# Softmax weights of mixer A's second-layer heads: turned by VectorE's 32x32 blocks and the DRAM instead of by TensorE, with their transfers on SyncE

## The chip, the cores and the metric

The kernel runs on one core of a Trainium2 chip. The metric is the device time of one execution in microseconds (us); lower is better. TensorE (PE) does the matrix products, VectorE (DVE), ScalarE (ACT) and GpSimd (POOL) the work between them, and SyncE (SP) issues the transfers (DMAs). Each engine takes its instructions in a fixed order, and an instruction that waits holds up those behind it on its engine. That order is set when the program is built, by a scheduler that sorts the instructions of each engine.

## The reference, cut to what matters

Two layers, each of a parallel mixer and a gated MLP, on 256 tokens of width 2048 in float32. In the mixer one projection gives queries, keys and values for mixer A (8 heads, windowed, a learned sink logit, 2 key/value heads) and mixer B (8 heads, neighbourhood attention with a bias), and a gate for each.

```
q, k normalised, a part of them rotated            # mixer A, per head of 128
s = q k^T * scale, masked to |i-j| <= 128
m = max(max_k s, sink)
p = exp(s - m);  p = p / (sum_k p + exp(sink - m)) # softmax weights, 256 x 256
o = p v
# mixer B: the same with a bias table in place of the mask and without the sink
x = x + gate * (out_proj(gA * proj_A(oA) + gB * proj_B(oB)))
x = x + gate * down(silu-gated, convolved up-projection)
```

For `o = p v` TensorE needs p with the keys on the partitions. The scores come out with the queries there, so each head's p (two tiles of 128 x 256) has to be turned.

## The kernel before, in words

**The weight stream.** The weights are read once, in units of 1 MB (16 blocks of 128 x 128; `unit_steps`, load `w` in L325 on SP). The pool of raw tiles holds four, shared with the rows `aw` of the adaptive-norm projection (L231), so a load is issued when an earlier unit's last reader is done. A unit is split in two halves: ACT casts a half to its upper part `hl[:, 0]` (L336), DVE subtracts for the lower part `hl[:, 1]` (L337), and the half lies in a ring of four. TensorE makes three products of each block (L355 to L357 for a block that gives features, L418 to L420 for one that gives tokens): the first, and for features the second too, needs only the upper part; the others need DVE's.

**Work beside the stream.** After each unit the stream calls `Paced.tick`: first the functions that `later(n, ...)` put off by n units, then the background jobs at their rates. The attention is such a job: `attention()` starts the eight heads of mixer A (`head_a`) and the eight of mixer B (`head_b`) in turn, and each of its steps moves every head that has begun by one `yield`. `ATT` is its rate for the two layers, `ATT_B` the rate once mixer A's projection is reached. Program order made in this way is what the scheduler starts from.

**A head** (`attend`, L643 on): scores `sc` on TensorE (L648, 6 products), the maxima with mask or bias on DVE (L651) and their negation `nm` (L656), exponentials with their sums on ACT (L659), for mixer A the sink's share (L662, L663), the reciprocal `ri` on DVE (L665), the scaling on ACT (L667), a `yield`, the turn, and then `po` on TensorE (L697), whose result goes to `oA` or `oB` through ACT and DVE (L699, L700).

**The turn.** By TensorE: four transposes to a PSUM tile `tp` (L689), which `split` brings to `pT` with a cast on ACT (L430) and a subtraction on DVE (L431) of 128 x 512. By blocks (`turned_blocks`): DVE transposes each of the two 128 x 256 tiles in blocks of 32 x 32 (L313) into two rows of storage; eight DMAs of 32 KB take them to a DRAM tile `pY` with the blocks exchanged (L316, issued by POOL); two DMAs of 128 KB on SP bring them back (`read_back`, L299); and `split` works on two pieces of 128 x 256. Each read-back is made to wait for `halved[0]`, the DVE split (L337) of the weight half that was emitted last at that point, so that SP's queue takes it no earlier. `BACK` says how many units the read-back is put off. `MOVED` lists, per layer, how many heads of mixers A and B are turned by blocks: in the kernel before none of the first layer, and of the second mixer B's eight.

**Also near:** q and k of later groups are normalised in the same stretch of the second layer: sums of squares on ACT (L588), `qss` on DVE (L481), the power on POOL (`qrs`, L482), `qn` on DVE (L597), transposes `qtp` on TensorE (L621), `packB` on ACT (L622). Each head's split of q, k and v is an ACT/DVE pair of 128 x 256 (L430, L431). The bias of a head of mixer B is loaded to its `p` by SP, 256 KB. `sc`, `po`, `tp` and `qtp` share one PSUM pool (`ax`).

Of the kernel before, what the change touches and what calls it, by code (L numbers as in the profile page):

```python
# [9 lines left out]
F32 = mybir.dt.float32  # L10
# [5 lines left out]
P = 128  # L16
L = 2
D = 2048
S = 256
# [12 lines left out]
BLOCK = 32  # L32
# [47 lines left out]

H_RATE = [2.7, 1.7]

ATT = [1.288, 0.4]
ATT_B = [0.21, 0.4]

SCORES_3 = (1,)

BACK = [3, 4]
MOVED = [(0, 0), (0, 8)]

ADA_ORDER = [[p * KC + k for k in range(KC) for p in ps] for ps in ((0, 1), (2,), (3, 4), (5,))]
ADA_ORDER = [i for part in ADA_ORDER for i in part]
# [47 lines left out]
def encoder(ctx: ExitStack, tc: tile.TileContext, a: dict, out: bass.AP):  # L140
    nc = tc.nc
# [18 lines left out]
    dram = pool("dram", 2, space=bass.MemoryType.DRAM)  # L160
# [126 lines left out]
    def once(fn):  # L287

        due = [fn]

        def run():
            if due:
                due.pop()()

        return run

    def read_back(dst, src):

        tc.add_manual_dep(nc.sync.dma_start(dst, src).ins, halved[0], BEHIND)  # L299

    def later(n, fn):

        if n == 0:
            fn()
        else:
            bg.defer(lambda: later(n - 1, fn))

    def turned_blocks(p, rows, n, tag):

        y = dram.tile([P, n, S], F32, name=tag, tag=tag)  # L310
        to = y[:].rearrange("(b i) n (t a j) -> t a i n b j", i=BLOCK, t=2, a=P // BLOCK)
        for t, row in enumerate(rows):
            nc.vector.transpose(out=row, in_=p[t])  # L313
            src = row.rearrange("p (n b j) -> p n b j", n=n, j=BLOCK)
            for a in range(P // BLOCK):
                nc.gpsimd.dma_start(to[t, a], src[a * BLOCK : (a + 1) * BLOCK])  # L316
        return y

    def unit_steps(l, u, by_halves=False):

# [106 lines left out]
    def split(dst, src, scale=None):  # L427

        if scale is None:
            nc.scalar.copy(dst[:, 0], src)  # L430
            nc.vector.tensor_tensor(out=dst[:, 1], in0=src, in1=dst[:, 0].bitcast(F32), op=ALU.subtract)  # L431
            return
        nc.scalar.activation(out=dst[:, 0], in_=src, func=AF.Copy, scale=scale)
        nc.vector.scalar_tensor_tensor(
            out=dst[:, 1], in0=src, scalar=scale, in1=dst[:, 0].bitcast(F32), op0=ALU.mult, op1=ALU.subtract
        )
# [192 lines left out]
    def in_halves(src, name, tag, yes):  # L629

        if not yes:
            return (src,)
        off = {"vh": ROW - OFF, "qh": 0, "kh": OFF}[tag]
        hl = at.tile([P, 2 * S + off], F32R, name=name, tag=tag, bufs=1)[:, off:]
        halves = hl.rearrange("p (i s) -> p i s", i=2) if len(src.shape) == 2 else hl.rearrange("p (i a s) -> p i a s", i=2, a=2)
        split(halves, src)
        return halves[:, 0], halves[:, 1]

    def by(x):

        return ((0, 0), (0, 1), (1, 0))[: 2 * len(x) - 1]

    def attend(q, k, v, p, mask, scale, sink, o, rows=None):  # L643

        sc = ax.tile([P, 2, S], F32, name="sc", tag="ax")
        for t in range(2):
            for i, j in by(q):
                nc.tensor.matmul(sc[:, t], q[i][:, t * P : (t + 1) * P], k[j], start=i + j == 0, stop=(i, j) == by(q)[-1])  # L648
        m = sm.tile([P, 2], F32, name="m", tag="m")
        for t in range(2):  # L650
            nc.vector.tensor_tensor_reduce(  # L651
                out=p[:, t], in0=sc[:, t], in1=mask[:, t], scale=scale, scalar=-3.0e38 if sink is None else sink,
                op0=ALU.add, op1=ALU.max, accum_out=m[:, t : t + 1],
            )
        nm = sm.tile([P, 2], F32, name="nm", tag="nm")
        nc.vector.tensor_scalar(out=nm[:], in0=m[:], scalar1=-1.0, scalar2=None, op0=ALU.mult)  # L656
        den = sm.tile([P, 2], F32, name="den", tag="den")
        for t in range(2):
            nc.scalar.activation(out=p[:, t], in_=p[:, t], func=AF.Exp, bias=nm[:, t : t + 1], accum_out=den[:, t : t + 1])  # L659
        if sink is not None:  # L660
            es = sm.tile([P, 2], F32, name="es", tag="es")
            nc.scalar.activation(out=es[:], in_=nm[:], func=AF.Exp, bias=sink)  # L662
            nc.vector.tensor_tensor(out=den[:], in0=den[:], in1=es[:], op=ALU.add)  # L663
        ri = sm.tile([P, 2], F32, name="ri", tag="ri")
        nc.vector.reciprocal(out=ri[:], in_=den[:])  # L665
        for t in range(2):
            nc.scalar.activation(out=p[:, t], in_=p[:, t], func=AF.Copy, scale=ri[:, t : t + 1])  # L667
        yield
        if rows is not None:
            rows = rows()  # L670
            y = turned_blocks([p[:, t] for t in range(2)], rows, 2, "pY")

            def back():
                for k in range(2):
                    read_back(rows[k], y[:, k])

            back = once(back)
            later(BACK[sink is None], back)
            yield
            yield  # L680
            back()
            pT = at.tile([P, 2, 2, S], F32R, name="pT", tag="pT", bufs=1)
            for k in range(2):
                split(pT[:, :, k], rows[k])
        else:
            tp = ax.tile([P, 2, S], F32, name="tp", tag="ax")
            for k in range(2):
                for t in range(2):
                    nc.tensor.transpose(tp[:, k, t * P : (t + 1) * P], p[:, t, k * P : (k + 1) * P], ident[:])  # L689
            pT = at.tile([P, 2, 2, S], F32R, name="pT", tag="pT", bufs=1)  # L690
            split(pT, tp[:])
        v = v()
        yield
        po = ax.tile([P, 512], F32, name="po", tag="ax")
        for i, j in by(v):
            for b in range(2):
                nc.tensor.matmul(po[:, :S], v[i][:, b], pT[:, j, b], start=i + j + b == 0, stop=i + b == 2)  # L697
        o = o()
        nc.scalar.copy(o[:, 0], po[:, :S])  # L699
        nc.vector.tensor_tensor(out=o[:, 1], in0=po[:, :S], in1=o[:, 0].bitcast(F32), op=ALU.subtract)  # L700
# [93 lines left out]
    def small(l):  # L794

        if l == 0:
            tables.extend((load(a["maskA"], [P, 2, S], "maskA"), load(a["cs"], [P, 2, 2, HALF], "cs")))
        cs = tables[1]
        gains = load(a["gains"][l], [P, 4], f"gains{l}", lay, tag="gains", bufs=1)
        rg = load(a["rg"][l], [P, 2, ROT], f"rg{l}", lay, tag="rg", bufs=1)  # L800
        sink = load(a["sink"][l], [P, HA], f"sink{l}", lay, tag="sink", bufs=1)
        cw = load(a["cw"][l], [P, 2 * FC, 4], f"cw{l}", lay, tag="cw", bufs=1)
        nc.vector.tensor_scalar(out=gains[:, 2:3], in0=gains[:, 2:3], scalar1=SCALE, scalar2=None, op0=ALU.mult)
        rots = []
        for w in range(2):
            rot = lay.tile([P, 4, 2, HALF], F32, name=f"rot{l}_{w}", tag=f"rot{w}", bufs=1)
            for i, (f, g) in enumerate(((0, 0), (1, 1), (0, 1), (1, 0))):
                nc.vector.tensor_tensor(
                    out=rot[:, i], in0=cs[:, f],
                    in1=rg[:, w, g * HALF : (g + 1) * HALF].unsqueeze(1).broadcast_to([P, 2, HALF]), op=ALU.mult,  # L810
                )
            rots.append(rot)

        return gains, sink, cw, rots

    for l in range(L):
# [41 lines left out]
        def head_a(i):  # L858
# [18 lines left out]
            def rows():  # L877
# [3 lines left out]
            yield from attend(  # L881
                q, k, v, p, tables[0], SCALE, sink[:, i : i + 1], lambda: oA[i], rows if i < MOVED[l][0] else None
            )

        def head_b(hb):
# [8 lines left out]
                q, k, lambda: in_halves(v[:, :, i * HEAD : (i + 1) * HEAD], f"vB{l}_{hb}", "vh", True), p, p, 1.0, None,  # L894
                lambda: oB_of(hb), (lambda: [b[:, 8 + i], b[:, i]]) if hb < MOVED[l][1] else None,
            )

        def oB_of(hb):
            if hb == 0:
                o = place("a", 12, F32R, f"oB{l}_{hb}")  # L900
                oB.extend(o[:, 2 * i : 2 * i + 2] for i in range(6))
            elif hb == 6:
                oB.extend(chunks_of(sp, "b0", 6, f"oB{l}_{hb}", 2))
            return oB[hb]
# [30 lines left out]
        for pi, (groups, gates) in enumerate(parts):  # L935
            last = pi == len(parts) - 1
            for g, part in enumerate(groups):
                have_h(part)
                pss = st.tokens(h, part)
                if pi == max(0, len(parts) - 2) and g == 0:  # L940
                    gains, sink, cw, rots = small(l)
                dst = packs[g // 3][:, 4 * (g % 3) : 4 * (g % 3) + 4]
                rows = dst.rearrange("p (t a) s -> p t (a s)", t=2)
# [25 lines left out]
                if g == 2:  # L969
                    bg.add(job, ATT[l])  # L970

# [29 lines left out]
        for tag in ("y0", "y1", "y2"):  # L1001
            t = place(tag, 4, F32, f"gb{l}_{tag}")
            gb += [t[:, i] for i in range(4)]
        for i in range(2):
            t = paired(F32, f"gb{l}_{i}")
# [56 lines left out]
        for gi, chunks in enumerate(FF_GROUPS):  # L1062
# [34 lines left out]
            for cs in sets:  # L1097
                fns = [lambda p, e=e, c=c: e(p, c) for c in cs for e in (g_evac, v_evac)]
                src = bare.chunks if gi == 0 and cs[0] < BARE[1] // 2 else bare.h
# [113 lines left out]
```

## Time and profile before

| what | before |
|---|---|
| device time, median of 3 runs (lowest to highest) | 2662.33 us (2660.89 to 2663.44) |
| device time of the profiled execution | 2661.44 us |
| its span, first to last instruction | 2659.3 us |
| mean granted TensorE clock | 1.000 |
| busy: PE, DVE, ACT, POOL | 2647.6, 2106.2, 1411.5, 75.0 us |
| HBM read, written | 697.13 MB, 4.19 MB |

The profiled execution takes 2.1 us more than its span and stands 0.9 us below the median of the three runs. The profile's rows name an engine, a line of the kernel, and the tile written and read; "PEld" is TensorE's loading of weights, "SPq" SyncE's queue, and "releaser" what an engine waited for. Matmuls overlap in their records, so the distance from start to start is what one costs.

### The profile page before, as it was taken

Reading aid. Unit: us, or ns where it says so; the run is one execution under the profiler, and the core shown is the slowest. Engines: PE = TensorE matmul, PEld = TensorE weight load, DVE = VectorE, ACT = ScalarE, POOL = GpSimd, SP = SyncE. Lnnn points to the kernel's source line nnn. Section 1 sums busy time; section 2 is a strip of 40 time slices with the busy share of each in tenths; the row PEclk is TensorE's granted clock in tenths of the full one; section 3 lists DMA queues with packets and bytes.
Section 4 is the critical chain, followed back from the end, with each engine's and each line's share of the span. In section 5 each row is a group of like instructions: output and inputs, shape, how many; then the busy total and the mean of one; then the engine's idle time right before and its main releaser. Section 6 shows DMA issues by size and latency. Waiting matters only on the chain.

```text
span 2659.3 us, 50973 instructions
## 1 busy us (share of the span) xinstructions
PE 2647.6 (100%) x21224; PEld 2562.6 (96%) x21224; DVE 2106.2 (79%) x2983; ACT 1411.5 (53%) x2292; POOL 75.0 (3%) x89
## 2 busy tenths in 40 slices
PE   9999999999999999999999999999999999999999
PEld 7888899999999999999998889999999999999999
DVE  8898998997987888788876666868888866655664
ACT  5445865456653554355554566555565445544553
POOL 0001100000000000000000001310000000000000
PEclk9999999999999999999999999999999999999999
DMA  9987789885777778788756666877747765555554
GB/s 365 349 327 297 264 300 351 321 311 212 290 295 286 296 290 287 288 297 296 295 205 256 236 229 238 299 264 261 278 179 287 297 251 191 191 197 194 196 191 143
DMA packets 106394, 704.63 MB, mean 265 GB/s; under 512 B 14001, under 2 KB 18353, under 8 KB 22321
## 3 DMA queue, kind: packets, MB, share of 16 engines
q1 hardware_dynamic: 104114, 699.27, 71.6%
q8 instruction: 166, 2.72, 0.4%
q0 software_dynamic: 2048, 2.10, 0.3%
q14 instruction: 66, 0.54, 0.1%
HBM read 697.13 MB, written 4.19 MB: 264 GB/s over the span
## 4 chain that ended last, share of the span: by engine, by line
PE 90%; DVE 5%; DMA 2%; ACT 1%; issue 1%; POOL 0%; DVEq 0%; ACTq 0%
PE ps L355 25%; PE ps L357 25%; PE ps L356 25%; PE ps_t L420 4%; PE ps_t L418 4%; PE ps_t L419 4%; DVE hl L337 2%; DVE aw L232 1%; DMA aw<-in_aw 1%; PE sc L648 1%; PE po L697 1%; ACT hl L336 1%; PE tp L689 0%; PE qtp L621 0%; DMA w<-in_ws 0%
## 5 line engine op out<-in xcount | busy, mean ns | idle before, releaser
L337 DVE TENSOR_TENSOR hl<-w,hl 128x1024 fp32r<-128x1024 f32 x928 | 1128.4, 1222 | 338.7 <-ACT hl L336 332.1
L336 ACT CAST hl<-w 128x1024 fp32r<-128x1024 f32 x928 | 970.6, 1049 | 738.3 <-PE ps L357 509.5
L355 PE MATMUL ps<-h,hl 128*128 128x256 f32 x3328 | 923.9, 278 | 1.3 <-DVE ya L979 0.6
L356 PE MATMUL ps<-h,hl 128*128 128x256 f32 x3328 | 921.1, 277 | 0.0
L357 PE MATMUL ps<-h,hl 128*128 128x256 f32 x3328 | 920.9, 277 | 0.0
L355 PEld LDWEIGHTS ps<-h,hl 128*128 128x128 f32 x3328 | 625.0, 188 | 2.4 <-DVE ya L979 0.8
L356 PEld LDWEIGHTS ps<-h,hl 128*128 128x128 f32 x3328 | 625.6, 188 | 0.4
L357 PEld LDWEIGHTS ps<-h,hl 128*128 128x128 f32 x3328 | 624.6, 188 | 0.0
L232 DVE CUSTOM_DVE_ANT_0 aw<-aw,cact,ab 128x2048 f32<-128x2048 f32 x189 | 443.5, 2347 | 61.1 <-DMA aw<-in_aw 60.4
L418 PE MATMUL ps_t<-hl,h 128*128 128x512 f32 x576 | 223.5, 393 | 2.1 <-ACT h L510 1.6
L419 PE MATMUL ps_t<-hl,h 128*128 128x512 f32 x576 | 225.1, 391 | 0.4
L420 PE MATMUL ps_t<-hl,h 128*128 128x512 f32 x576 | 224.6, 391 | 0.0
L1058 DVE SCALAR_TENSOR_TENSOR u<-ps,cw,u 128x255 f32<-128x255 f32 x304 | 146.2, 481 | 66.5 <-ACT u L1056 62.5
L1056 ACT ACTIVATE u<-ps,cw 128x256 f32<-128x256 f32 x152 | 85.7, 564 | 183.1 <-PE ps L357 183.0
L357 PE MATMUL ps<-merged,hl 128*128 128x256 f32 x512 | 141.8, 277 | 0.2 <-DVE hl L337 0.2
L355 PE MATMUL ps<-merged,hl 128*128 128x256 f32 x512 | 141.7, 277 | 0.0
L356 PE MATMUL ps<-merged,hl 128*128 128x256 f32 x512 | 141.7, 277 | 0.0
L356 PE MATMUL ps<-act_o,hl 128*128 128x256 f32 x512 | 141.6, 277 | 0.0
L357 PE MATMUL ps<-act_o,hl 128*128 128x256 f32 x512 | 141.6, 276 | 0.0
L355 PE MATMUL ps<-act_o,hl 128*128 128x256 f32 x512 | 141.4, 277 | 0.0
L418 PEld LDWEIGHTS ps_t<-hl,h 128*128 128x128 f32 x576 | 108.0, 188 | 25.5 <-ACT h L510 2.6
L419 PEld LDWEIGHTS ps_t<-hl,h 128*128 128x128 f32 x576 | 108.2, 188 | 24.0 <-DVE hl L337 2.1
(235 smaller groups left out, 4657.8 us busy)
## 6 DMA issues: line engine op xcount, KB each, us to landing
w<-in_ws SPq DMA_DIRECT2D x463, 1024.0 KB, 5.0
aw<-in_aw SPq DMA_DIRECT2D x189, 1024.0 KB, 6.1
p<-in_bias SPq DMA_DIRECT2D x16, 256.0 KB, 4.4
x<-in_xT SPq DMA_DIRECT2D x4, 512.0 KB, 5.5
aw_o<-in_aw SPq DMA_DIRECT2D x2, 1024.0 KB, 13.1
pY<-packB POOLq DMA_DIRECT2D x64, 32.0 KB, 4.2
packB<-pY SPq DMA_DIRECT2D x16, 128.0 KB, 2.7
out<-x SPq DMA_DIRECT2D x16, 128.0 KB, 2.6
```

Of the source, the lines that this page charges most:

```text
L232: nc.vector.tensor_tensor_reduce(out=raw[:], in0=raw[:], in1=cact[:], scale=1.0, scalar=ab[:, i : i + 1], op0=ALU.mult, op1=ALU.add, accum ...
L336: nc.scalar.copy(hl[:, 0], r)
L337: halved[0] = nc.vector.tensor_tensor(out=hl[:, 1], in0=r, in1=hl[:, 0].bitcast(F32), op=ALU.subtract).ins.name
L355: nc.tensor.matmul(out, hi, act[0], start=first, stop=False)
L356: nc.tensor.matmul(ps[:, :S], hi, act[1], start=False, stop=False)
L357: nc.tensor.matmul(out, lo, act[0], start=False, stop=last)
L418: nc.tensor.matmul(ps[:], xh, hi, start=kc == kcs[0], stop=False)
L419: nc.tensor.matmul(ps[:], xh, lo, start=False, stop=False)
L420: nc.tensor.matmul(ps[:], xl, hi, start=False, stop=kc == kcs[-1])
L648: nc.tensor.matmul(sc[:, t], q[i][:, t * P : (t + 1) * P], k[j], start=i + j == 0, stop=(i, j) == by(q)[-1])
L1056: nc.scalar.activation(out=u, in_=ps, func=AF.Identity, scale=w[:, 1:2], bias=w[:, 3:4])
L1058: nc.vector.scalar_tensor_tensor(out=u[:, to], in0=ps[:, of], scalar=w[:, j : j + 1], in1=u[:, to], op0=ALU.mult, op1=ALU.add)
```

## The change

In the second layer, mixer A's eight heads are turned by blocks as well (`MOVED`). Their eight DMAs to the DRAM go out on SP through `read_back`, each tied to the last emitted weight split, and put off by one unit (`later(1, ...)`); the two read-backs are put off by `BACK[0]` = 3 units. Mixer B's DMAs to the DRAM stay on POOL. The storage for a turned head of mixer A is the head's own query tile `qTa[:, i]`, and a spare tile from a pool of two. The number of `yield`s between the turn's start and its end becomes 2 for mixer A and 3 for mixer B (`STEPS`), instead of 2; the attention job's rate in the second layer goes from 0.4 to 0.46 (`ATT`). Line numbers below the changed functions move by 5 to 13.

```diff
--- before.py
+++ after.py
@@ -80,13 +80,14 @@
 
 H_RATE = [2.7, 1.7]
 
-ATT = [1.288, 0.4]
+ATT = [1.288, 0.46]
 ATT_B = [0.21, 0.4]
 
 SCORES_3 = (1,)
 
 BACK = [3, 4]
-MOVED = [(0, 0), (0, 8)]
+STEPS = [2, 3]
+MOVED = [(0, 0), (8, 8)]
 
 ADA_ORDER = [[p * KC + k for k in range(KC) for p in ps] for ps in ((0, 1), (2,), (3, 4), (5,))]
 ADA_ORDER = [i for part in ADA_ORDER for i in part]
@@ -294,6 +295,11 @@
 
         return run
 
+    def by_gpsimd(outs):
+
+        for to, src in outs:
+            nc.gpsimd.dma_start(to, src)
+
     def read_back(dst, src):
 
         tc.add_manual_dep(nc.sync.dma_start(dst, src).ins, halved[0], BEHIND)
@@ -307,14 +313,13 @@
 
     def turned_blocks(p, rows, n, tag):
 
-        y = dram.tile([P, n, S], F32, name=tag, tag=tag)
+        y, outs = dram.tile([P, n, S], F32, name=tag, tag=tag), []
         to = y[:].rearrange("(b i) n (t a j) -> t a i n b j", i=BLOCK, t=2, a=P // BLOCK)
         for t, row in enumerate(rows):
             nc.vector.transpose(out=row, in_=p[t])
             src = row.rearrange("p (n b j) -> p n b j", n=n, j=BLOCK)
-            for a in range(P // BLOCK):
-                nc.gpsimd.dma_start(to[t, a], src[a * BLOCK : (a + 1) * BLOCK])
-        return y
+            outs += [(to[t, a], src[a * BLOCK : (a + 1) * BLOCK]) for a in range(P // BLOCK)]
+        return y, outs
 
     def unit_steps(l, u, by_halves=False):
 
@@ -668,17 +673,25 @@
         yield
         if rows is not None:
             rows = rows()
-            y = turned_blocks([p[:, t] for t in range(2)], rows, 2, "pY")
+            y, outs = turned_blocks([p[:, t] for t in range(2)], rows, 2, "pY")
+            if sink is None:
+                steps = [lambda: by_gpsimd(outs)]
+                steps[0]()
+            else:
+                steps = [once(lambda: [read_back(*o) for o in outs])]
+                later(1, steps[0])
 
             def back():
                 for k in range(2):
                     read_back(rows[k], y[:, k])
 
-            back = once(back)
-            later(BACK[sink is None], back)
-            yield
-            yield
-            back()
+            steps.append(once(back))
+            later(BACK[sink is None], steps[1])
+            for _ in range(STEPS[sink is None]):
+                yield
+            if sink is not None:
+                steps[0]()
+            steps[1]()
             pT = at.tile([P, 2, 2, S], F32R, name="pT", tag="pT", bufs=1)
             for k in range(2):
                 split(pT[:, :, k], rows[k])
```

## Prediction

> **What bounds the kernel now.** I read the page first: busy shares, the chain that ended last, the groups.
>
> ```profile
> PE 2647.6 (100%) x21224; PEld 2562.6 (96%) x21224; DVE 2106.2 (79%) x2983; ACT 1411.5 (53%) x2292; POOL 75.0 (3%) x89
> ...
> PE 90%; DVE 5%; DMA 2%; ACT 1%; issue 1%; POOL 0%; DVEq 0%; ACTq 0%
> ...
> L337 DVE TENSOR_TENSOR hl<-w,hl 128x1024 fp32r<-128x1024 f32 x928 | 1128.4, 1222 | 338.7 <-ACT hl L336 332.1
> L336 ACT CAST hl<-w 128x1024 fp32r<-128x1024 f32 x928 | 970.6, 1049 | 738.3 <-PE ps L357 509.5
> ```
>
> PE is never short of work. ACT's casts wait mostly for PE to free the ring of halves: the weights are ahead of PE. Next the stretches of mixer A's second-layer heads, where the change acts.
>
> ```profile
> 1620.00:1640.00 20.00, 19.94 (x175) 19.73 (x174) 13.80 (x24) 13.53 (x28) 0.00 (x0) 1.00 0.76 282
> sum 180.00, PE 179.94 PEld 159.65 DVE 121.60 ACT 112.94 POOL 14.31; mean PE 19.99 PEld 17.74 DVE 13.51 ACT 12.55 POOL 1.59
> ```
>
> From 1480 to 1660 PE is idle for 0.06 us of 180 (first number behind the stretch's length). So what leaves PE's queue here is gained whole, and every new wait of PE is lost whole: no slack absorbs it.
>
> **What it removes.** 32 transposes. The timeline of PE at one head:
>
> ```profile
> 1600.62 0.87 PE L697 MATMUL po<-pT,vA 128*128 128x256 f32 x6
> 1601.34 0.60 PE L689 MATMUL tp<-ident,p 128*128 128x128 f32 x4
> 1601.69 0.94 PE L648 MATMUL sc<-kA,qA 128*128 128x256 f32 x6
> 1602.47 0.40 PE L418 MATMUL ps_t<-hl,h 128*128 128x512 f32 x1
> ```
>
> Four transposes hold PE from 1601.34 to 1601.69, 0.35 us; eight groups are 2.8 us, and with the 0.06 of idleness and some longer groups I take **-3.0 us**. The built program's order of instructions has these 32 gone from PE and nothing else there added, so the change does what it says.
>
> **What it adds, away from PE.** The groups of 1500 to 1780 (mean ns behind the busy time):
>
> ```profile
> L316 POOL DMA_DIRECT2D pY<-packB x64 | 39.4, 618 | 96.6 <-DVE packB L313 51.8 <-issue 44.4
> L659 ACT ACTIVATE p<-p,nm 128x256 f32<-128x256 f32 x32 | 16.0, 501 | 5.7 <-DVE nm L656 5.7
> ...
> L588 ACT ACTIVATE qsq<-ps_t 128x128 f32<-128x128 f32 x24 | 6.6, 275 | 1.5 <-PE ps_t L420 1.1
> ...
> L313 DVE STREAM_TRANSPOSE packB<-p 128x256 f32<-128x256 f32 x16 | 6.4, 430 | 1.7 <-ACT p L667 1.7
> ...
> L659 ACT ACTIVATION_READ_ACCUMULATOR p<-p,nm 128x1 f32 x32 | 6.0, 187 | 0.0
> L431 DVE TENSOR_TENSOR pT<-tp,pT 128x512 fp32r<-128x512 f32 x8 | 5.5, 684 | 0.1
> L431 DVE TENSOR_TENSOR pT<-packB,pT 128x256 fp32r<-128x256 f32 x14 | 5.3, 419 | 0.0
> L430 ACT CAST pT<-packB 128x256 fp32r<-128x256 f32 x14 | 5.1, 414 | 1.1 <-DMA packB<-pY 1.1
> ...
> L622 ACT ACTIVATE packB<-qtp,gains 128x512 f32<-128x512 f32 x8 | 5.1, 688 | 0.0
> L482 POOL TENSOR_TENSOR qrs<-qss,mhalf 128x8 f32<-128x8 f32 x3 | 4.9, 1637 | 118.3 <-DVE qss L481 118.3
> ...
> L430 ACT CAST pT<-tp 128x512 fp32r<-128x512 f32 x8 | 4.7, 593 | 0.0
> L588 ACT ACTIVATION_READ_ACCUMULATOR qsq<-ps_t 128x1 f32 x24 | 4.7, 197 | 0.0
> ...
> L597 DVE TENSOR_TENSOR qn<-ps_t,qrs 128x512 f32<-128x512 f32 x6 | 3.9, 686 | 5.4 <-POOL qrs L482 5.4
> ...
> L699 ACT CAST oA<-po 128x256 fp32r<-128x256 f32 x8 | 3.0, 373 | 0.0
> ...
> L481 DVE TENSOR_SCALAR qss<-qss 128x8 f32<-128x8 f32 x3 | 0.5, 167 | 1.0 <-ACT qsq L588 1.0
> ```
>
> Per head DVE gets two block transposes (0.86) and two splits of 0.42 for one of 0.68: +1.0 us, 8 in all. ACT gets 2 x 0.41 for 0.59: +0.24. In the stretches above DVE is busy 13.5 of 20 us and ACT 12.6, so the work itself is hidden; uncovered, it would cost 8 + 2. POOL is unchanged.
>
> SP gets 64 issues and 16 read-backs, and now they stand between the loads:
>
> ```profile
> 1567.57 4.94 SPq L325 DMA_DIRECT2D w<-in_ws  x3
> 1579.32 0.33 SPq L231 DMA_DIRECT2D aw<-in_aw  x1
> ```
>
> and the landings of the outgoing DMAs (L316), of the read-backs (L299) and of a bias:
>
> ```profile
> DMA to landing us min/median/max: 1.9/4.2/6.5
> ```
> ```profile
> DMA to landing us min/median/max: 2.0/2.7/4.8
> ```
> ```profile
> p<-in_bias SPq DMA_DIRECT2D x16, 256.0 KB, 4.4
> ```
>
> A strided issue on SP isn't in the trace: between 0.33 (a plain SP issue) and 0.62 (POOL's, for the same shape); I take 0.33, which is SP's own. Eight are 2.6 to 5 us per head. A head has about 12 (24 token products of 0.227 make a unit of 5.4 us, and the job steps 0.46 times a unit), so issuing alone delays nothing. But SP waits in order: the outgoing DMAs and the read-backs each wait for a split, the read-backs also for the outgoing ones to land (4.2), and behind them stand `w_39`, `w_40`, `w_42`, `w_44` and `w_47` and the biases.
>
> **What it moves.** This decides. The DVE order before, the same head:
>
> ```profile
> 1601.96 1.23 DVE L337 TENSOR_TENSOR hl<-w,hl 128x1024 fp32r<-128x1024 f32 x1 [1.55 <-ACT hl L336]
> 1603.10 0.42 DVE L700 TENSOR_TENSOR oA<-po,oA 128x256 fp32r<-128x256 f32 x1
> ...
> 1604.03 0.48 DVE L651 CUSTOM_DVE_ANT_0 p<-sc,maskA,sink 128x256 f32<-128x256 f32 x1
> ...
> 1604.84 0.42 DVE L431 TENSOR_TENSOR qA<-packA,qA 128x256 fp32r<-128x256 f32 x1
> 1605.17 0.16 DVE L656 TENSOR_SCALAR nm<-m 128x2 f32<-128x2 f32 x1
> ```
>
> A weight split goes first, the scores' maxima behind it. Counting the order of before, every half is split behind PE results that are at least 5.5 us of PE work older than PE's first use of that half; mostly 8. In the changed order, five units lose this lead. There PE's order has `sc` directly ahead of the unit's first product, and DVE's order has the maxima of those same scores ahead of the unit's split. PE must wait while DVE and ACT do, from the end of `sc`, what stands between, less the 0.2 to 0.45 us of products that need no lower half. Distances from start to start (maxima 0.8 a pair, a 128x256 split 0.34, `nm` and `ri` 0.1, a weight split 1.22, its cast 1.05):
>
> - unit 36: `sc` of head 4 waits for `packB` (0.69), which ACT has behind the cast of 36 (1.05): **1.7**. Head 5's and 7's queries and 37, 39: **1.4**, an allowance.
> - unit 40: scores of heads 6 and 7 stand together before it. DVE: maxima 6 and `qA`, `oA`, `vA` splits end 0.75 after `sc` 7, then maxima 0.8, `nm`, `ri` and `den` 0.3, split 1.2, less 0.45: **2.6**. Unit 41 follows with 6.3 us of DVE work for 5.4 of products: **1.0**.
> - unit 42 (first scores of mixer B): maxima 0.8, `qB` and `nm` 0.4, two exponentials with their sums on ACT 1.3, cast 1.05, split 1.2, less 0.45: 4.3; its bias stands behind head 4's read-backs and head 5's eight DMAs on SP, 0.9 more: **5.2**.
> - unit 44: DVE's split stands behind `qn`. The eight squares on ACT (8 x 0.47, with a 0.37 and two 0.41 casts between, begun 1.4 before `sc` ends) end 3.5 us after `sc`, then `qss` 0.17, POOL 1.64, two `qn` 1.3, `ri` 0.1, split 1.2, less 0.6 of PE's own: **7.3**.
> - unit 47: `po` of head 7 and two scores of mixer B; `oA` 0.7, `pT` 0.7, maxima 0.8, `qB`, `nm`, `kB` 0.8, split 1.2, less 1.9 of PE's own: **2.3**.
>
> Sum 21.5. Behind 47 the order has its lead of 5.5 us again. The faster job and the third step of mixer B only spread it; its earlier end brings PE, which has no gap there, nothing: 0, or with the lead lost once more there, 2.3 as at 47.
>
> Net: +21.5 - 3.0 = +18.5. On the profiled execution, 2661.4 + 18.5 = **2680 us**; the median of before stands 0.9 above that execution, which I leave in the range.
>
> A rule against the change: the Trainium skill, "VectorE: DVE Perf Modes", section "Rules for kernel authors", leaves a 128x128 transpose to TensorE where PSUM will do. By that rule the move gains nothing; by the row of L689 it gains the 3.0 us. The sum above has the row's.
>
> **Rivals.**
>
> 1. *The order costs nothing*, not slower. In the first layer of this trace a lower half came just in time:
>
> ```profile
> 356.63 1.22 DVE L337 TENSOR_TENSOR hl<-w,hl 128x1024 fp32r<-128x1024 f32 x1
> ...
> 357.77 0.28 PE L355 MATMUL ps<-oA,hl 128*128 128x256 f32 x1
> 357.91 0.39 PE L357 MATMUL ps<-oA,hl 128*128 128x256 f32 x1
> ```
>
> The split ends at 357.85, its first product starts at 357.91, and PE had no gap: five products of this and later halves had been put ahead. So a lost lead is no wait by itself. It would be 2661.4 - 3.0 = 2658.4, if at units 36 to 47 the fill covers DVE's work. Against it: at unit 40 only two such products stand ahead, 0.45 us against 3.1. It decides by whether PE's stalls there stay under 3 us in sum.
> 2. *SP's round trips are longer and compound.* If landings are at their longest (6.5 for 4.2 outward, and 4.8 for 2.7 back) each of five heads without lead adds up to 4.4 us, 22 in all; with two thirds of that, 2695. For it: each waits behind another on one queue; against it: in the page's row of L336 casts wait for PE's ring, not for loads.
> 3. *PE's clock falls after the long stalls* at 42 and 44. Rows of the start, the granted clock behind the POOL column:
>
> ```profile
> 0.00:5.00 5.00, 2.26 (x3) 1.15 (x4) 0.31 (x7) 1.49 (x2) 1.38 (x7) 1.00 0.51 149
> 35.00:40.00 5.00, 4.40 (x18) 2.98 (x17) 3.93 (x6) 3.27 (x5) 0.00 (x0) 1.00 0.81 308
> ```
>
> With 2.74 us of PE idle in the first stretch the clock stays 1.00, so no such fall is seen; longer gaps aren't in the trace. If the first 3 us after each of the two ran at half speed: 3 more, 2683. The Trainium skill, "TensorE: Matmul & The Clock Gate", section "HAM oscillation — how this bites in real kernels", names gaps above about 3.4 us for it; by that rule only these two stalls qualify.
> 4. *A larger gain*, below 2656: nothing but the 0.06 us of idleness is there to win beside the transposes.
>
> **How the numbers follow.** Forecast 0.56 (2680), rival 1 0.21 (2658), rival 2 0.11 (2695), rival 3 0.08 (2683), rival 4 0.04. A measurement of this kernel tells about 0.2%, 5.3 us, from no change: faster 0.04, same 0.21, slower 0.75. The likeliest case's own range is 2668 (unit 44's chain and one other stall alone, 7.3 + 2.6, less 3.0) to 2689 (SP's strided issues at POOL's price on four heads, 4 x 8 x 0.29). Rival 1 and most of rival 2 belong in the range of 8 in 10: 2657 to 2696.
>
> **What would show it.** Right: PE's idle time between 1480 and 1640 grows from 0.06 to about 20 us, in waits of 2 to 7 us on ACT's and DVE's `hl` and on `packB`, the longest at `qtp` and unit 44 behind `qrs`; L689 keeps 64 transposes; PE's busy time falls by about 3. Wrong: PE's idle time there is under 3 us (rival 1), the waits end on `w` or `pY` transfers (rival 2), the clock is under 1.00 in a stretch (rival 3).

## The result, and the profile after

The changed kernel takes 2677.16 us (median of 6 runs, 2675.79 to 2678.41), the kernel before 2661.61 us beside it (6 runs, 2660.46 to 2663.44): a ratio of 1.0058, 95% interval 1.0045 to 1.0071, or 15.5 us more. The profiled execution took 2678.05 us, its span 2676.3 us: 17.0 more than before's.

The head of the page, and TensorE's waits from 1480 to 1700 us (what waited, for what; us in all, times, longest). In the kernel before this list is empty.

```profile
PE 2652.6 (99%) x21192; PEld 2564.1 (96%) x21192; DVE 2112.0 (79%) x3007; ACT 1409.9 (53%) x2300; POOL 75.8 (3%) x89
```

```profile
PE ps_t L423 <- ACT hl L341: 5.0, 2, 3.4
PE qtp L626 <- DVE qn L602: 4.5, 1, 4.5
PE ps_t L424 <- DVE hl L342: 1.1, 2, 0.5
PE sc L653 <- DVE qA L436: 0.3, 1, 0.3
PE ps L360 <- ACT hl L341: 0.3, 1, 0.3
PE ps L362 <- DVE hl L342: 0.3, 1, 0.3
PE sc L653 <- ACT packB L627: 0.2, 1, 0.2
```

They sum to 11.7 us. The 32 transposes are gone (21224 to 21192 products). But PE's busy time went up by 5.0 us where 3.0 less was due (and its idle time by 12.0, from 11.7 to 23.7 us of the span). The windows tell why: the first number behind the stretch's length is PE's busy time, and the third from the right is the granted clock.

```profile
1580.00:1600.00 20.00, 17.56 (x76) 14.06 (x75) 12.72 (x31) 11.39 (x27) 0.00 (x0) 0.91 0.52 175
1600.00:1620.00 20.00, 15.81 (x73) 12.77 (x71) 11.11 (x22) 9.72 (x27) 0.00 (x0) 0.91 0.72 257
1620.00:1640.00 20.00, 15.82 (x117) 15.83 (x118) 11.28 (x22) 11.52 (x26) 11.61 (x17) 0.83 0.67 195
1640.00:1660.00 20.00, 19.32 (x159) 18.36 (x159) 17.03 (x34) 12.58 (x29) 2.45 (x4) 1.00 0.96 373
```

TensorE's clock fell. Of 60 us, 0.09 x 20 + 0.09 x 20 + 0.17 x 20 = 7.0 us of clock are missing, some of them while PE stood still. Waits 11.7, clock up to 7.0, transposes -3.0: 15.7 of the 17.0 us by which the span grew. The rest is not placed.

Now the place of the longest but one wait, unit 42. SyncE's timeline ahead of it (start, duration, what was issued; `x4` are four in a row):

```profile
1575.68 0.60 SPq L330 DMA_DIRECT2D w<-in_ws  x1
1576.39 0.37 SPq L232 DMA_DIRECT2D aw<-in_aw  x1
1576.86 0.37 SPq L330 DMA_DIRECT2D w<-in_ws  x1
1589.55 0.33 SPq L305 DMA_DIRECT2D packA<-pY  x1
1589.92 0.43 SPq L305 DMA_DIRECT2D spare<-pY  x1
1590.40 2.54 SPq L305 DMA_DIRECT2D pY<-packA  x4
1592.98 2.57 SPq L305 DMA_DIRECT2D pY<-spare  x4
1596.36 0.55 SPq L902 DMA_DIRECT2D p<-in_bias  x1
1596.95 0.91 SPq L330 DMA_DIRECT2D w<-in_ws  x2
```

and SyncE's longest waits from 1560 to 1640 (for the landing of an outgoing DMA it waited once, 0.7 us):

```profile
SPq L305 <- DVE hl L342: 24.2, 3, 12.1
SPq L305 <- DVE packB L319: 21.1, 2, 11.9
```

After the load of unit 41 at 1576.86, SyncE does nothing for 12 us: the next in its queue is head 4's read-back, tied to the split of unit 40, which ends at 1589.5. Then come 0.8 us of read-backs, 5.1 us of outgoing DMAs and a bias, and only at 1596.95 the load of unit 42, with 4.9 us to land. In the kernel before, the group of three loads at 1567.57 that the prediction shows holds the same unit, and PE used it at 1595.2. Here PE needed it at 1601.6. The order of the engines at that point:

```profile
1600.91 0.37 ACT L712 CAST oA<-po 128x256 fp32r<-128x256 f32 x1 [7.42 <-PE po L710]
1601.32 0.42 DVE L713 TENSOR_TENSOR oA<-po,oA 128x256 fp32r<-128x256 f32 x1 [5.03 <-ACT oA L712]
1601.66 0.41 DVE L656 CUSTOM_DVE_ANT_0 p<-sc,p 128x256 f32<-128x256 f32 x1
...
1602.88 0.51 ACT L664 ACTIVATE p<-p,nm 128x256 f32<-128x256 f32 x1 [0.49 <-DVE nm L661]
...
1603.88 1.98 ACT L341 CAST hl<-w 128x1024 fp32r<-128x1024 f32 x2
...
1604.94 2.36 DVE L342 TENSOR_TENSOR hl<-w,hl 128x1024 fp32r<-128x1024 f32 x2 [0.77 <-ACT hl L341]
1604.96 0.73 PE L423 MATMUL ps_t<-hl,h 128*128 128x512 f32 x2 [3.37 <-ACT hl L341]
```

The chain is the one forecast (`sc`, maxima, exponentials, cast, split), but look at the brackets: ACT had been idle for 7.4 us and DVE for 5.0. They weren't too busy to make the half earlier; until 1601.9 its weights hadn't landed. The cast then comes 2.0 us after the landing, without a gap behind the exponentials. So in this execution ACT's fixed order ends the wait, and the same order with an earlier landing would end it no sooner. Units 40 and 44 are alike: their first casts begin 4.3 and 3.1 us after the landing. Why the order came out so is asked below.

### The profile page after: what moved, and what is told of

It is laid out like the page before. It is cut to its first block, busy times and chain, and to the rows that moved or that the text cites. A ratio compares the mean times of both kernels' runs of the same rounds, so it can differ in the third digit from the quotient of the medians.

```text
span 2676.3 us, 51034 instructions
## 1 busy us (share of the span) xinstructions
PE 2652.6 (99%) x21192; PEld 2564.1 (96%) x21192; DVE 2112.0 (79%) x3007; ACT 1409.9 (53%) x2300; POOL 75.8 (3%) x89
## 4 chain that ended last, share of the span: by engine, by line
PE 89%; DVE 5%; ACT 2%; DMA 2%; issue 1%; POOL 0%; ACTq 0%; DVEq 0%; SPq 0%; POOLq 0%
PE ps L360 25%; PE ps L362 25%; PE ps L361 25%; PE ps_t L424 4%; PE ps_t L425 4%; PE ps_t L423 4%; DVE hl L342 2%; DVE aw L233 1%; ACT hl L341 1%; DMA w<-in_ws 1%; DMA aw<-in_aw 1%; PE sc L653 1%; PE po L710 1%; POOL qrs L487 0%; ACT qsq L593 0%
```

## The experiments

Theory 1: SyncE's queue, where tied read-backs and eight slow issues per head now stand ahead of the weight loads, makes the loads late. Theory 2: DVE's and ACT's added work, and scores' maxima placed ahead of weight splits, make PE wait. Theory 3: the faster attention job.

**outs_pool.** For mixer A too, `by_gpsimd(outs)` at once:

```diff
-            if sink is None:
-                steps = [lambda: by_gpsimd(outs)]
-                steps[0]()
-            else:
-                steps = [once(lambda: [read_back(*o) for o in outs])]
-                later(1, steps[0])
+            steps = [once(lambda: by_gpsimd(outs))]
+            steps[0]()
```

> The changed kernel with one part undone: mixer A's eight outgoing DMAs per head go out on POOL at once, as mixer B's do; read-backs, rate and steps stay. Theory 1 (SP's one queue holds the weight loads behind the tied read-backs and the eight strided issues): the loads get their lead back, PE's idle time between 1480 and 1700 us falls from 14 us to under 1, the clock stays 1.00, and the time is that of before less the 3.0 us of transposes, about 2658.5. Theory 2 (DVE's and ACT's added work and the place of the maxima ahead of the splits make PE wait): nothing changes in that, about 2677. Theory 3 (the faster attention job does it): about 2677.

(The idle time that it puts at 14 us is 11.7 by the list above.) 2671.56 us (2668.62 to 2677.51), ratio 1.0042 (1.0029 to 1.0054). A miss: only a third of the loss went. The profiled execution is the slowest of the five, 2677.51, and 3.5 us of its waits lie outside the stretch, at 1330 and 2120. Inside, PE's waits moved:

```profile
PE ps L362 <- DVE hl L342: 2.9, 1, 2.9
PE sc L653 <- ACT packB L627: 2.4, 1, 2.4
PE qtp L626 <- DVE oA L709: 0.9, 1, 0.9
PE ps_t L424 <- DVE hl L342: 0.3, 1, 0.3
```

and the reason stands in what POOL's 128 issues waited for (us, times), next to 44.4 us for 64 in the kernel before:

```profile
  issue: 86.6, 52
```

POOL takes 0.61 us per DMA and stops between them for nothing that the profile names. So a head's eight are spread over 10 to 13 us, and the read-backs wait in SyncE's queue for them, again with loads behind.

**no_dma, rate_only.** Without any transfer of mixer A, and with the rate and steps alone:

```diff
-                steps = [once(lambda: [read_back(*o) for o in outs])]
+                steps = [lambda: None]
...
-            steps.append(once(back))
+            steps.append(once(back if sink is None else lambda: None))
```

```diff
-MOVED = [(0, 0), (8, 8)]
+MOVED = [(0, 0), (0, 8)]
```

> The changed kernel without mixer A's second-layer transfers: the eight outgoing DMAs and the two read-backs of each head are left out, so the blocks are transposed in place but not exchanged, and the splits read them at once. All DVE and ACT work of the change stays. Theory 1: about 2658.5. Theory 2: about 2677, since the added work of the engines is all there. Theory 3: about 2677.

> The change's rate and steps alone (0.46 a unit, three steps for mixer B); mixer A's heads are turned by TensorE as before. Theory 1 and 2: as before, 2661 to 2663. Theory 3: most of the 15.5 us, 2670 or more.

no_dma: 2661.22 us (2656.80 to 2664.03), ratio 0.9994 (0.9985 to 1.0003); its profiled span is 2655.0 and PE has no wait from 1480 to 1700. That execution is the fastest of the ten, and half of them took over 2662, so the 3 us of the transposes don't show in the median, where theory 1 expected them. rate_only: 2661.41 us, ratio 1.0005 (0.9996 to 1.0015). All of DVE's and ACT's new work is in no_dma, so the added work falls as the cause; theory 3 falls too. The transfers cost the time. The other half of theory 2, the maxima ahead of the splits, isn't tested by this: without the transfers the scheduler built another order (see the table below).

**only_back, no_back.** The two kinds of transfer apart:

```diff
-                steps = [once(lambda: [read_back(*o) for o in outs])]
+                steps = [lambda: None]
...
-                    read_back(rows[k], y[:, k])
+                    read_back(rows[k], y[:, k] if sink is None else a["ws"][1, k][:, :S])
```

```diff
-            steps.append(once(back))
+            steps.append(once(back if sink is None else lambda: None))
```

> The counterpart: mixer A's read-backs stay on SP with their ties, but bring 128x256 of the weights in place of the turned block (the eight outgoing DMAs and the exchange are left out, and the heads' results are not the reference's). Theory 1: two plain issues, 0.8 us a head, and no landing to wait for; the loads keep their lead: 2658 to 2661. Rival (the tie to a later split alone stops SP long enough): 2665 or more.

> The changed kernel without mixer A's read-backs in the second layer: the eight outgoing DMAs of each head stay on SP, tied as they are, but nothing is brought back and the splits read the transposed blocks at once (the exchange of blocks is left out). Theory 1 (SP's eight strided issues, 0.61 us each, 5.1 us a head behind the tied split, hold up the weight loads): PE still waits at units 41 and 44, 5 to 10 us in all, and the time is 2664 to 2672. Rival (the wait for the round trip before po costs the time): 2658 to 2660.

only_back: 2657.73 us (2656.23 to 2660.86), ratio 0.9987 (0.9978 to 0.9996): below before by 3.4 us (1.1 to 5.9), about the 3 us of the transposes. PE's stretch with the tied read-backs on SyncE:

```profile
1600.00:1620.00 20.00, 20.00 (x150) 18.96 (x149) 15.65 (x31) 14.96 (x41) 4.12 (x5) 1.00 0.66 229
1620.00:1640.00 20.00, 20.00 (x179) 20.00 (x178) 13.47 (x22) 12.61 (x27) 6.23 (x11) 1.00 0.73 250
```

no_back: 2668.35 us (2667.38 to 2669.25), ratio 1.0025 (1.0015 to 1.0035), with 7.1 us of PE's waits from 1480 to 1700, the longest of them at unit 44:

```profile
PE ps L360 <- ACT hl L341: 3.5, 1, 3.5
PE qtp L626 <- DVE qn L602: 1.0, 1, 1.0
```

So the tied read-backs alone do no harm. With the outgoing DMAs and no read-backs the time is 7.2 us above before, and 7.7 against no_dma, from which no_back differs by these DMAs alone (each time against the kernel before beside it). With both it is 15.5.

**w_pool.** The loads of units 33 to 50 taken off SyncE instead:

```diff
-            nc.sync.dma_start(raw[:], a["ws"][l, u])
+            (nc.gpsimd if l == 1 and 33 <= u <= 50 else nc.sync).dma_start(raw[:], a["ws"][l, u])
```

> The changed kernel with the weight loads of units 33 to 50 of the second layer issued by POOL; the outgoing DMAs and read-backs stay on SP, tied as they are. Theory 1: with the loads past that queue PE's idle time there falls under 2 us and the time to 2658 to 2662 (POOL's issue may cost a little). If instead the transfers' own round trip holds up PE (po waits for a read-back), the time stays at 2670 to 2677.

2670.51 us (2667.30 to 2675.43), ratio 1.0034 (1.0024 to 1.0044). A miss as well: the weights were past the queue, but the `aw` rows were not. DVE waited 8.2 us for one, in its fixed order, with two splits and head 5's `oA` behind:

```profile
1632.43 2.35 DVE L233 CUSTOM_DVE_ANT_0 aw<-aw,cact,ab 128x2048 f32<-128x2048 f32 x1 [8.23 <-DMA aw<-in_aw]
...
1634.71 2.35 DVE L342 TENSOR_TENSOR hl<-w,hl 128x1024 fp32r<-128x1024 f32 x2
...
1637.46 0.66 PE L626 MATMUL qtp<-ident,qn 128*128 128x128 f32 x4 [3.67 <-DVE oA L713]
```

**all_pool, pool_back5.** From outs_pool on: the read-backs on POOL too, or later on SyncE.

```diff
-                    read_back(rows[k], y[:, k])
+                    if sink is None:
+                        read_back(rows[k], y[:, k])
+                    else:
+                        nc.gpsimd.dma_start(rows[k], y[:, k])
```

```diff
-BACK = [3, 4]
-STEPS = [2, 3]
+BACK = [5, 4]
+STEPS = [3, 3]
```

> Mixer A's transfers of the second layer wholly on POOL: the eight outgoing DMAs and the two read-backs of each head; none of them is in SP's queue. Theory 1, in its wider form (what costs the time is any transfer that waits in SP's queue ahead of weight loads: in outs_pool the read-backs waited there for POOL's slow outgoing DMAs): SP's loads are as in the kernel before, PE has under 1 us of idle time from 1480 to 1700, and the time is 2658 to 2660. Rival: the round trip itself is too long on POOL, and DVE's and ACT's splits of the turned weights hold up the weight splits behind them: 2668 or more, as in outs_pool, with PE's waits on hl and packB again.

> outs_pool with the read-backs of mixer A put off by five units instead of three and three steps instead of two. Theory 1, wider form: the outgoing DMAs have landed when SP reaches the read-backs, so SP passes them at once, and the time falls from outs_pool's 2671.6 to 2658 to 2662. Rival (POOL's outgoing DMAs take DVE's time, or hold up qrs): it stays at 2668 to 2674.

all_pool: 2673.32 us (2668.22 to 2674.21), ratio 1.0036 (1.0023 to 1.0050). pool_back5: 2680.18 us (2677.85 to 2684.30), ratio 1.0069 (1.0056 to 1.0083). Both miss theory 1 in its wider form: with SyncE relieved, POOL's own work is late. In all_pool DVE waits for `qrs`, which POOL has behind eight outgoing DMAs, and DVE has the next weight split behind `qn`:

```profile
1623.59 1.23 POOL L301 DMA_DIRECT2D pY<-spare  x2
1625.22 1.22 POOL L301 DMA_DIRECT2D pY<-spare  x2 [0.40 <-issue]
1626.46 1.66 POOL L487 TENSOR_TENSOR qrs<-qss,mhalf 128x8 f32<-128x8 f32 x1
```

```profile
1628.15 1.29 DVE L602 TENSOR_TENSOR qn<-ps_t,qrs 128x512 f32<-128x512 f32 x2 [8.64 <-POOL qrs L487]
1629.36 1.22 DVE L342 TENSOR_TENSOR hl<-w,hl 128x1024 fp32r<-128x1024 f32 x1
```

The first fence is POOL's timeline, the second DVE's: 8.6 us idle, and the split only behind. In pool_back5 the same wait is 5.9 us long.

**outs_act3, half3.** The eight DMAs on ACT's queue, and four on SyncE with four on POOL; read-backs on SyncE put off by four units, three steps.

```diff
+            steps = [once(lambda: [nc.scalar.dma_start(*o) for o in outs] if sink is not None else by_gpsimd(outs))]
+            steps[0]()
```

```diff
+                by_gpsimd(outs[4:])
+                steps = [once(lambda: [read_back(*o) for o in outs[:4]])]
+                later(1, steps[0])
```

> A version meant to keep the gain: mixer A's eight outgoing DMAs go out on ACT's queue right behind the block transposes, the read-backs stay on SP, put off by four units, with three steps. POOL's qrs and SP's loads are past the eight issues. If SP's issues and POOL's delays are the whole cost: 2658 to 2661. Rival: eight strided issues at 0.6 us are 5 us of ACT per head of 12, on an engine that is busy 12.6 of 20 us there, and the casts of the weights come late: 2666 or more.

> A dose: of mixer A's eight outgoing DMAs per head four stay on SP (tied, put off by one unit) and four go out on POOL at once; read-backs on SP put off by four units, with three steps. SP's strided issues per head fall from 5.1 to 2.5 us and POOL's from 5 to 2.5 against outs_pool. If the loss grows with the strided issues that one queue takes ahead of its other work: 2658 to 2664, and below before only if both queues keep their other work in time. If any such issue on SP or POOL costs the same wherever it stands: 2669 to 2677.

outs_act3: 2681.59 us (2679.85 to 2683.09), ratio 1.0077 (1.0064 to 1.0090), by the rival's price: 0.62 us an issue on ACT, with exponentials and casts behind. The weights of unit 41 lay there 19.8 us before their first cast, and PE waited 1.9 us for it all the same.

```profile
L677 ACTq DMA_DIRECT2D pY<-packA x32: 577/621/1699, 1507.3 to 1606.1; - x32
```

half3: 2676.97 us (2676.37 to 2682.03), ratio 1.0062 (1.0049 to 1.0076). The dose gave nothing: one wait of 11.4 us, where mixer A's projection reads `oA`, holds most of it (its waits from 1640 to 1690). SyncE's queue stood at a read-back of mixer B that waited for POOL's DMAs, an `aw` row behind it came 10.2 us late, and DVE had `oA` behind that row:

```profile
DVE aw L233 <- DMA aw<-in_aw: 16.5, 2, 10.2
...
PE ps L361 <- DVE oA L714: 11.4, 1, 11.4
```

**heads_0_3.** Four heads alone: `MOVED = [(0, 0), (4, 8)]`.

> The change for mixer A's heads 0 to 3 of the second layer alone; heads 4 to 7 are turned by TensorE. Half of the transposes go (1.5 us). The waits at units 40 to 47 belong to the read-backs and outgoing DMAs of heads 3 to 7, so theory 1 expects only the small waits of units 36 and 37 (0.4 us in the changed kernel): 2660 to 2662. If each moved head costs the same, half of the 15.5 us stays: about 2669.

2660.66 us (2658.61 to 2665.39), ratio 0.9998 (0.9989 to 1.0007): the first four cost nothing that shows. Where the two routes meet, head 3 takes the other group's values here, with the same work. So the loss isn't a price per head: it comes in when heads 4 to 7 are moved as well. (These four alone were not run.)

**fill.** Products that nothing reads, put into the waits:

```diff
+        if rows is not None:
+            warm(fill)
```

> The changed kernel with idle products added on TensorE (identity times identity into a tile that nothing reads): 5 behind the scores of head 7 of mixer A, 12 and 16 behind those of heads 0 and 1 of mixer B, some 1.3, 3 and 4 us in the three waits of 1.8, 3.5 and 4.6 us. They shorten no wait. If PE's idleness makes the clock fall to half for 3 to 7 us after each (4 us of slow products, 1 to 2 more inside the waits): the clock stays 1.00 and the time falls to 2671 to 2673, with the waits as they are. If the clock has another cause, it stays 0.997 and the time is 2677 or above.

2677.66 us (2674.80 to 2680.86), ratio 1.0058 (1.0046 to 1.0071): no gain in the median, and no run came down to the 2671 to 2673 expected. The profiled execution is the fastest of the five, 2674.80, with the clock at 1.00 in the three stretches that had 0.91, 0.91 and 0.83:

```profile
1580.00:1600.00 20.00, 18.39 (x102) 15.24 (x101) 13.90 (x37) 12.59 (x30) 0.00 (x0) 1.00 0.54 184
1600.00:1620.00 20.00, 18.23 (x108) 15.57 (x107) 11.88 (x25) 11.08 (x35) 2.15 (x2) 1.00 0.75 272
1620.00:1640.00 20.00, 17.98 (x152) 17.35 (x153) 12.05 (x16) 9.11 (x14) 9.56 (x16) 1.00 0.69 209
```

The other four had a mean clock of 0.998 to 0.999 (0.997 in every run of the changed kernel) and took 2676.66 to 2680.86. That the clock follows PE's idleness is borne out by the profiled execution; what it costs isn't settled: the filling takes some of the time itself.

**The order, read from the traces.** The time from the start of a unit's first cast on ACT to PE's first product of that unit, in us (casts and products counted off in order; a small number means that nothing is in hand):

| unit | 40 | 41 | 42 | 43 | 44 |
|---|---|---|---|---|---|
| before | 10.8 | 10.8 | 8.0 | 9.0 | 9.8 |
| changed | 1.1 | 4.6 | 1.1 | 6.1 | 3.2 |
| no_back | 6.5 | 1.1 | 3.6 | 5.8 | 1.1 |
| no_dma | 10.2 | 10.3 | 9.0 | 9.4 | 9.4 |
| w_pool | 10.2 | 10.3 | 9.0 | 9.4 | 9.3 |
| outs_pool | 10.2 | 10.3 | 9.0 | 9.4 | 9.4 |
| half3 | 10.2 | 10.3 | 9.4 | 9.4 | 9.4 |
| outs_act3 | 3.5 | 1.1 | 1.1 | 6.8 | 1.1 |

The lead is lost where the outgoing DMAs of all eight heads stand on SyncE ahead of the weight loads (changed, no_back), and where ACT, which makes the casts, issues them (outs_act3). It is kept in the others, though DVE and ACT turn and split as much there. So the order that the prediction read goes with the transfers. And a kept lead isn't enough: w_pool, outs_pool and half3 lose 9 to 16.5 us with it.

## Why the prediction was right, and where it wasn't

It forecast 2680 us, 18.5 more; measured were 15.5 more. The sign, the size and the places hold. The size is in part luck, by two errors that cancel: the waits were put 9.8 us too high, and the clock, which the sum left out, took up to 7.0. What was to show it came out mixed: PE's idle time grew by 12 us and not by 20, PE's busy time rose by 5.0 where it was to fall by 3, and the longest wait did come at `qtp`, behind `qrs`.

- **The transposes, -3.0.** Right, as far as the runs tell: only_back, which has no outgoing DMAs, stands 3.4 us below before.
- **DVE's and ACT's added work, 0.** Right: no_dma has it, and PE no wait from 1480 to 1700.
- **"Issuing alone delays nothing", at 0.33 us an issue.** The price is wrong: the strided issue took 0.61 us on SyncE:

```profile
L305 SPq DMA_DIRECT2D pY<-packA x32: 581/610/1032, 1513.2 to 1629.9; - x32
```

  The upper bound was the nearer one, since POOL's row was of the same shape. And no_back puts the outgoing DMAs, without any read-back, at 7.7 us over no_dma: they come in a block behind the split that releases them, when loads are due. Ahead of unit 41's load SyncE stood 8.8 us at one tie and then issued the blocks of two heads, 5.1 us each. So they do delay the loads, though what of it is the issue and what the tie isn't separated.
- **"This decides": the place of maxima ahead of splits.** Right for the changed kernel. The waits came at units 40, 42, 44 and 47 as listed, and the long ones ended through the chains as listed. But it isn't the whole cause: the table shows that this order goes with transfers ahead of the loads, and that kernels which keep their lead lose 10 us (outs_pool) and 16.5 (half3). The count held engines' results against PE's need and left landings out.
- **The sum of waits, 21.5.** Measured 11.7. Unit 42 was 3.4 and 0.5 (5.2 forecast), unit 44 4.5 (7.3), 36 to 39 0.2 in place of 3.1, 41 none, 47 under 1 (2.3); unit 40 was 1.6 and 0.5 (2.6).
- **Rival 3, the clock, 8 in 100 and 3 us.** It happened, as part of the likeliest case, after the short waits at unit 40 too, and took up to 7.0 us. It made up for most of the waits that were put too high.
- **Rival 2, SyncE's round trips.** Half right. SyncE's queue does make the loads late, and "casts wait for PE's ring, not for loads" was an argument from the kernel before, where nothing of this stood ahead of the loads. But it wasn't by long landings: from 1560 to 1640 SyncE's read-backs and outgoing DMAs waited 45.3 us for DVE, where their ties are, and 0.7 us for an outgoing DMA to land.

Left open: what part of the loss each of the tie, the landing and the issues has when all three are there (7.2 without the read-backs, 15.5 with all), and what part the order has against late weights, since no run keeps the one and changes the other; what stops POOL between its DMAs; and whether a version that keeps the 3 us exists. None of the six placements tried does; clear below before lies only_back alone, which leaves the outgoing DMAs out.

## What to carry to other kernels

When work is moved off the engine that bounds the kernel, its transfers take a place in somebody's queue, and each queue here had something behind it that PE needed soon: weights and `aw` rows on SyncE, `qrs` on POOL, casts on ACT. Price the issue by the row of the same shape, not by the row of the same engine, and ask for each of a queue's next entries when it was due. An order in which every result stands early enough says nothing of transfers that land late.

## What the runs showed of the hardware

TensorE's clock fell to half after short waits. Rows of one microsecond each in the changed kernel, at unit 40:

```profile
1585.00:1586.00 1.00, 0.00 (x0) 0.00 (x0) 0.99 (x6) 1.00 (x4) 0.00 (x0) 1.00 0.16 66
1586.00:1587.00 1.00, 0.44 (x2) 0.30 (x2) 0.64 (x3) 1.00 (x3) 0.00 (x0) 1.00 0.00 0
1587.00:1588.00 1.00, 0.47 (x3) 0.18 (x2) 1.00 (x2) 1.00 (x2) 0.00 (x0) 1.00 0.00 0
1588.00:1589.00 1.00, 1.00 (x4) 0.82 (x5) 0.83 (x2) 1.00 (x4) 0.00 (x0) 0.81 0.00 0
1589.00:1590.00 1.00, 1.00 (x4) 0.76 (x3) 1.00 (x2) 1.00 (x6) 0.00 (x0) 0.50 0.00 0
...
1591.00:1592.00 1.00, 1.00 (x3) 0.74 (x3) 1.00 (x4) 1.00 (x2) 0.00 (x0) 0.50 0.68 184
```

PE was idle for 1.6 and 0.5 us within 3 us, no longer gap, and some 2 us after the end of the first, at 1586.56, the clock fell; it stood at 0.50 to 1592. The Trainium skill, "TensorE: Matmul & The Clock Gate", section "HAM oscillation — how this bites in real kernels", names gaps above about 3.4 us; here two shorter ones were enough. One can be enough: in outs_pool the wait of 2.4 us for `packB`, which ended at 1564.56, went with 0.68, 0.50, 0.50 and 0.61 in the four such rows from 1564, while a wait of 2.1 us in half3, ended at 1621.65, left the clock at 1.00. The waits of 3.4 and 4.5 us at units 42 and 44 were followed by half clock too.
